# Column sums of block 3's norms: wide matmuls in four column groups instead of narrow ones

## The chip, the cores and the metric

The kernel runs on one core of a Trainium2 chip. The metric is the device time of one execution in microseconds (us). The core has a matmul engine (TensorE, PE in the profile; its weight loads are PEld), a vector engine (VectorE, DVE), a scalar engine (ScalarE, ACT), GpSimd (POOL) and SyncE (SP), which here only issues DMAs. The engines run side by side, each works through its own instructions in the order in which the program has them, and they wait for one another by semaphores. TensorE's results go to PSUM, eight banks of 128 partitions by 512 floats; everything else lies in SBUF.

## The reference

Three transformer blocks run one after the other on 512 tokens of width 1024, all in float32. The change touches the third. What of it matters here:

```python
def rms_norm_3(x, g):
    y = x32 * lax.rsqrt(jnp.mean(x32 * x32, axis=-1, keepdims=True) + EPS)
    return y.astype(x.dtype) * g

def layer_norm(x, g, b):
    mu = jnp.mean(x32, axis=-1, keepdims=True)
    xc = x32 - mu
    var = jnp.mean(xc * xc, axis=-1, keepdims=True)
    ...

    z = h @ w_in                                   # 1024 -> 4800
    c_q, c_kv, k_r, u_glu, gate_logits = jnp.split(z, IN_OFFSETS, axis=-1)
    q = (rms_norm_3(c_q, q_norm) @ w_uq)...        # c_q: 384 channels
    c_kv_n = rms_norm_3(c_kv, kv_norm)             # c_kv: 256 channels
    ...                                            # keys, values, 8 heads of causal attention
    u = a * jax.nn.sigmoid(b)                      # from u_glu
    u = lax.conv_general_dilated(u, conv_w, ...)   # 31 taps, depthwise, 1024 channels
    u = jax.nn.silu(layer_norm(u, conv_ln_g, conv_ln_b))
    y_conv = u @ w_pw2 + b_pw2
    merged = sigmoid(g_attn) * y_attn + sigmoid(g_conv) * y_conv
```

The program keeps these activations with channels in the partitions (tiles of 128 channels by 512 tokens), so a mean over channels is a sum over partitions and over tiles.

## The kernel before

The middle of block 3 is a mixture of several streams written as Python generators: `lat_p` (the 38 column blocks of `h @ w_in`; tile `pj`, 24 matmuls per block), `conv` (the 31 taps, each one VectorE instruction on a PSUM accumulator `cv`; result `uc`, L2146 and L2149), `mla_pre` (rope of the shared key, the two latent norms, the values `v`), `projs` and `heads` (per-head projections `sp`, scores `at`, transposed probabilities `pT`, outputs `ao`) and `conv_ln` (the LayerNorm after the convolution, then SiLU, written as the pair `uhh`/`uhl`). `run` interleaves them: each generator yields how many ns it thinks its last piece takes, and the one with the least sum goes next. A list scheduler under the language then orders each engine's instructions by readiness in its own model, so the order that runs is neither the text nor the yields alone.

A big product is three matmuls on float32r halves (`mm3`: high by high, high by low, low by high). The weights of `pj` come by DMA as `w`; ScalarE makes the high half `wh` (L442) and, in this stage, GpSimd the low half `wl` (L443), one unit for 12 matmuls.

The channel sums are made by `col_stat` (L2161). For each of the four groups of 128 tokens and each tile, it takes the 128x128 float32 piece of the tile as the stationary operand and a column pair of ones as the moving one, and accumulates into two columns of `cs`. That is four matmuls per tile: 8 for the key-value latents (2 tiles `ckn`), 12 for the query latents (3 tiles `cqn`), 32 for the sum of `uc` and 32 for the sum of its squares `ucq`. Each float32 matmul shows as two records in the trace. The sums land with tokens in the partitions, as 128x4.

For the latents (`col_rsqrt`, L2176) VectorE then turns the sum into mean plus epsilon (`cm`, L2186), GpSimd raises it to the power -1/2 (`cr`, L572), and `col_spread` (L2168) broadcasts the factor over all partitions by four matmuls (`cb`). VectorE multiplies each latent by `cb` (L2196). `conv_ln` does the same with its own lines (mean `mu` L2334, `cb`, subtraction L2337, squares L2342, `cm` L2346, `cr`, `cb`, product L2353).

Of the kernel before, what the change touches and what calls it, by code (L numbers as in the profile page):

```python
# [11 lines left out]
F32 = mybir.dt.float32  # L12
# [3 lines left out]
AF = mybir.ActivationFunctionType  # L16
OP = mybir.AluOpType
# [5 lines left out]
TT = 4  # L23
# [291 lines left out]
def kernel(ctx: ExitStack, tc: tile.TileContext, A, out):  # L315
    nc = tc.nc
    V, P, SC, PE = nc.vector, nc.gpsimd, nc.scalar, nc.tensor

    glob = ctx.enter_context(tc.tile_pool(name="glob", bufs=1))
# [5 lines left out]
    def T(name, dt=F32, n=512):  # L325
        return heap.tile([128, n], dt, name=name, tag="t")
# [4 lines left out]
    def SM(name, n, dt=F32):  # L331
        assert n <= 32
        return glob.tile([128, n], dt, name=name, tag="sm", bufs=24)

    def PS(name="ps"):
        return psum.tile([128, 512], F32, name=name, tag="ps")
# [10 lines left out]
    def con(n, i=0, w=None):  # L347
        o, ww = _COFF[n]
        w = ww if w is None else w
        return cons[:, o + i:o + i + w]  # L350
# [13 lines left out]
    def tok(t):  # L364
        return slice(128 * t, 128 * t + 128)
# [117 lines left out]
    for g in G3:  # L483
        n = (b + g + 1) // 2 - (b + 1) // 2
# [8 lines left out]
    def mm(ps, a, b, start, stop, **kw):  # L493
        PE.matmul(ps, a, b, start=start, stop=stop, **kw)  # L494
# [76 lines left out]
    def pow_half(y, m, n):  # L571
        P.tensor_tensor(y, m, mhalf[:, :n], op=OP.pow)  # L572
# [101 lines left out]
    for i, nm in enumerate(("c", "c_ctx")):  # L674
        cs = SM("cs", 8)
# [182 lines left out]
    for o in range(0, _NM, 512):  # L858
        a = T("mf")
# [447 lines left out]
    for e in range(NE):  # L1307
# [29 lines left out]
        for q in range(8):  # L1337
            w, rel = ws.raw()
            for kk in range(2):
                f = 2 * q + kk  # L1340
                p, c, j = f // 8, (f // 4) % 2, f % 4
# [9 lines left out]
        a = T("yg")  # L1351
# [803 lines left out]
    del xb, h2f, fp, first  # L2155
    table("sigmoid_and_others")

    ones = glob.tile([128, 2], F32, name="ones")
    P.memset(ones, 1.0)

    def col_stat(tiles, n):  # L2161

        ps = PS("cs")
        for t in range(TT):
            for i, a in enumerate(tiles):
                mm(ps[:, 2 * t:2 * t + 2], a[:, tok(t)], ones, t == 0 and i == 0,
                   t == TT - 1 and i == n - 1, skip_group_check=True)
        return ps[:, 0:8:2]  # L2168

    def col_spread(y):  # L2170

        ps = PS("cb")
        for t in range(TT):
            mm(ps[:, tok(t)], y[:, t:t + 1].to_broadcast([128, 128]), ident, True, True)
        return ps

    def col_rsqrt(tiles, width, eps, name):
        sq = []
        for a in tiles:
            b = T(name)  # L2180
            SC.activation(b, a, AF.Square)
            sq.append(b)
            yield 1400
        m, r = SM("cm", 4), SM("cr", 4)
        cs = col_stat(sq, len(sq))
        V.tensor_scalar(m, cs, 1.0 / width, eps, op0=OP.mult, op1=OP.add)  # L2186
        pow_half(r, m, 4)
        yield 3000
        res = col_spread(r)
        yield 1000  # L2190
        return res

    def latent_norm(tiles, width, gname, name, dst):
        rb_ = yield from col_rsqrt(tiles, width, EPS, name)
        for i, a in enumerate(tiles):
            V.scalar_tensor_tensor(a, a, vec(gname, i), rb_, op0=OP.mult, op1=OP.mult)  # L2196
            dst[i] = split(a, name, eng=P)
            yield 1500
# [130 lines left out]
    def conv_ln():  # L2329

        yield from slow(CV2, cv.rest())
        us_ = [uc[i] for i in range(8)]
        mu = SM("mu", 4)
        V.tensor_scalar(mu, col_stat(us_, 8), -1.0 / D, None, op0=OP.mult)  # L2334
        mb = col_spread(mu)
        for i in range(8):
# [3 lines left out]
        for a in us_:  # L2340
# [3 lines left out]
            yield 700  # L2344
        m, r = SM("cm", 4), SM("cr", 4)
        V.tensor_scalar(m, col_stat(sq, 8), 1.0 / D, EPS, op0=OP.mult, op1=OP.add)  # L2346
        del sq
        pow_half(r, m, 4)
# [106 lines left out]
```

## Time and profile before

| | us |
|---|---|
| median of 3 runs | 3111.37 (3109.46 to 3112.55) |
| the profiled execution | 3115.6 |
| its span in the trace | 3113.8 |
| TensorE busy | 2848.8 (91%) |
| VectorE busy | 1281.0 (41%) |
| ScalarE busy | 785.6 (25%) |
| GpSimd busy | 471.2 (15%) |

The profiled execution is 4.2 us over the median, and its span is 1.8 us shorter than its own time. The mixture of block 3 that holds all four norms lies between about 2325 and 2660 us of the span. Busy shares over the whole span say nothing of it; a stage is read by its own windows, where the granted clock of TensorE (1.00 is 2.4 GHz, 0.50 is 1.2 GHz) stands beside the busy time of each engine.

### The profile page before, as it was taken

The numbers are of one execution on the slowest core, as the hardware profiler recorded it, in microseconds if no ns is written. First come the engines' busy times: TensorE is split into PE (matmuls) and PEld (weight loads), VectorE is DVE, ScalarE is ACT, GpSimd is POOL, SyncE is SP. The second block draws the span as 40 slices with busy tenths as digits, with TensorE's granted clock in tenths as the row PEclk, the third lists the DMA queues.
The fourth block names the chain that finished last, engine by engine and source line by source line (L and its number), as shares of the span: only waits on it lengthen the run. The fifth ranks groups of instructions, "written<-read, shape, count | busy, mean of one in ns | idle before, by whom it ended". The sixth has DMA issues, their size and how long they took to land.

```text
span 3113.8 us, 35071 instructions
## 1 busy us (share of the span) xinstructions
PE 2848.8 (91%) x13954; PEld 1874.6 (60%) x13954; DVE 1281.0 (41%) x2363; ACT 785.6 (25%) x1623; POOL 471.2 (15%) x437
## 2 busy tenths in 40 slices
PE   7989979998888888887997899999998989999999
PEld 4866564442222222224875688888886766788887
DVE  4157551111112111114476653333798554453334
ACT  3233220100000000004332332223433233442322
POOL 1034230000000000002310111000253232310100
PEclk8989979999999999998998999999998989999999
DMA  6123538999999999994200122222322112422321
GB/s 259 68 82 129 219 140 337 392 419 420 419 420 419 419 420 420 420 419 187 83 27 1 69 95 95 102 95 88 125 95 84 65 38 88 176 82 102 108 83 67
DMA packets 99012, 605.29 MB, mean 194 GB/s; under 512 B 11008, under 2 KB 11136, under 8 KB 31008
## 3 DMA queue, kind: packets, MB, share of 16 engines
q1 hardware_dynamic: 98640, 602.39, 49.4%
q8 instruction: 110, 1.80, 0.2%
q0 software_dynamic: 208, 0.66, 0.1%
q14 instruction: 54, 0.44, 0.0%
HBM read 592.52 MB, written 10.49 MB: 194 GB/s over the span
## 4 chain that ended last, share of the span: by engine, by line
PE 60%; DMA 24%; DVE 11%; POOL 2%; issue 2%; ACT 2%; SPq 0%; POOLq 0%; DVEq 0%; ACTq 0%
PE pj L494 25%; PE pn L494 15%; DMA wb<-in_w_up_dram 9%; DMA w<-in_w_up_dram 5%; DMA wb<-in_w_down_dram 4%; PE pg L494 4%; DMA w<-in_w_down_dram 4%; DVE cv L2146 3%; PE py L494 2%; PE at L494 2%; PE sp L494 1%; PE xs L494 1%; PE pc L494 1%; PE ao L494 1%; PE kv L494 1%
## 5 line engine op out<-in xcount | busy, mean ns | idle before, releaser
L443 DVE TENSOR_TENSOR wl<-w,wh 128x512 fp32r<-128x512 f32 (+1 forms) x422 | 297.8, 749 | 204.1 <-ACT wh L442 156.1
L494 PE MATMUL pg<-wb,xs 128*64 128x512 f32 x1184 | 283.2, 607 | 38.4 <-DMA wb<-in_w_up_dram 21.4
L442 ACT CAST wh<-w 128x512 fp32r<-128x512 f32 (+1 forms) x516 | 292.0, 617 | 99.3 <-PE pn L494 94.4
L494 PE MATMUL pg<-w,xs 128*64 128x512 f32 x824 | 197.9, 604 | 28.6 <-DMA w<-in_w_up_dram 15.4
L572 POOL TENSOR_TENSOR r<-m,mhalf 128x1 f32<-128x1 f32 x46 | 31.0, 676 | 1213.1 <-DVE m L618 1206.6
L494 PEld LDWEIGHTS pg<-wb,xs 128*64 128x64 f32 x1184 | 76.9, 138 | 220.9 <-issue 126.9
L494 PE MATMUL pn<-wh,fh 128*128 128x512 f32 x432 | 168.1, 389 | 0.0
L494 PE MATMUL pn<-wh,fl 128*128 128x512 f32 x432 | 168.1, 389 | 0.0
L494 PE MATMUL pn<-wl,fh 128*128 128x512 f32 x432 | 168.1, 389 | 0.0
L494 PE MATMUL py<-wb,hidT 128*64 128x512 f32 x600 | 142.6, 601 | 26.4 <-DMA wb<-in_w_down_dram 26.4
L2146 DVE SCALAR_TENSOR_TENSOR cv<-glua,vecs,cv 128x482 f32<-128x482 f32 (+27 forms) x232 | 165.1, 736 | 4.0
L443 POOL TENSOR_TENSOR wl<-w,wh 128x512 fp32r<-128x512 f32 x94 | 124.9, 1347 | 166.7 <-ACT wh L442 153.3
L494 PEld LDWEIGHTS pg<-w,xs 128*64 128x64 f32 x824 | 52.4, 136 | 153.7 <-issue 84.4
L494 PE MATMUL pj<-h2fh,wh 128*128 128x512 f32 (+1 forms) x376 | 141.4, 378 | 2.5 <-ACT h2fh L644 2.5
L494 PE MATMUL pj<-h2fl,wh 128*128 128x512 f32 (+1 forms) x376 | 141.7, 377 | 0.0
L494 PE MATMUL pj<-h2fh,wl 128*128 128x512 f32 (+1 forms) x376 | 141.6, 377 | 0.0
L1335 DVE TENSOR_TENSOR sg<-sg,pg 128x512 f32<-128x512 f32 x16 | 11.0, 687 | 292.6 <-PE pg L494 292.6
L494 PE MATMUL pj<-h3h,wh 128*128 128x512 f32 (+1 forms) x336 | 129.6, 386 | 0.6 <-ACT h3h L644 0.6
L494 PE MATMUL pj<-h3l,wh 128*128 128x512 f32 (+1 forms) x336 | 127.0, 378 | 0.6 <-DVE h3l L646 0.6
L494 PE MATMUL pj<-h3h,wl 128*128 128x512 f32 (+1 forms) x336 | 126.8, 377 | 0.0
L1352 DVE SCALAR_TENSOR_TENSOR yg<-py,gsl,g2h 128x512 f32<-128x512 f32 x16 | 12.0, 751 | 271.5 <-PE py L494 271.5
L494 PE MATMUL py<-w,hidT 128*64 128x512 f32 x424 | 101.7, 602 | 20.9 <-DMA w<-in_w_down_dram 20.9
(610 smaller groups left out, 5736.4 us busy)
## 6 DMA issues: line engine op xcount, KB each, us to landing
wb<-in_w_gate_dram SPq DMA_DIRECT2D x75, 1024.0 KB, 19.9
wb<-in_w_down_dram SPq DMA_DIRECT2D x75, 1024.0 KB, 19.9
wb<-in_w_up_dram SPq DMA_DIRECT2D x73, 1024.0 KB, 19.9
w<-in_w_down_dram SPq DMA_DIRECT2D x53, 1024.0 KB, 19.9
w<-in_w_up_dram SPq DMA_DIRECT2D x52, 1024.0 KB, 19.9
w<-in_w_gate_dram SPq DMA_DIRECT2D x51, 1024.0 KB, 19.9
w<-in_w_in_dram SPq DMA_DIRECT2D x35, 1024.0 KB, 5.0
w<-in_w_ff_dram SPq DMA_DIRECT2D x30, 1024.0 KB, 4.8
```

The source lines that it names most:

```text
L442: SC.copy(hi, src)
L443: (eng or V).tensor_tensor(lo, src, hi.bitcast(F32), op=OP.subtract)
L494: PE.matmul(ps, a, b, start=start, stop=stop, **kw)
L572: P.tensor_tensor(y, m, mhalf[:, :n], op=OP.pow)
L1335: V.tensor_tensor(sg, sg, pu, op=OP.mult)
L1352: V.scalar_tensor_tensor(a, py, gsl[:, e:e + 1], g2h, op0=OP.mult, op1=OP.mult)
L2146: V.scalar_tensor_tensor(acc[:, sh:], a[:, :512 - sh], w[j], acc[:, sh:], op0=OP.mult, op1=OP.add)
```

## The change

`col_stat` makes the sums in two steps. First each tile is the moving operand (512 tokens wide) and a 128x32 tile of ones the stationary one; tile i writes the 32 PSUM partitions from 32*(i mod 4), so that four tiles use the four column groups of the array, and tiles 4 to 7 accumulate onto tiles 0 to 3. All 32 rows of a group hold the same sum. ScalarE copies `cs` to an SBUF tile `csum`. Then four narrow matmuls per sum, with `csum` stationary and `half2` moving (0.5 in every 16th partition, so two rows of each group count half each), bring the result to 128x4 as before, in a second bank (`cs2`). In `col_rsqrt` the step `cm` is split: ScalarE scales, GpSimd adds epsilon. One yield there is 5000 instead of 3000. `half2` is made once by GpSimd at the start of its queue.

```diff
-    ones = glob.tile([128, 2], F32, name="ones")
+    ones = glob.tile([128, 32], F32, name="ones")
     P.memset(ones, 1.0)
 
+    half2 = glob.tile([128, 2], F32, name="half2")
+    P.tensor_scalar(half2, con("eye16", 0, 1).to_broadcast([128, 2]), 0.5, None, op0=OP.mult)
+
     def col_stat(tiles, n):
         ps = PS("cs")
+        g = min(n, 4)
+        for i, a in enumerate(tiles):
+            c = 32 * (i % 4)
+            mm(ps[c:c + 32, :], ones, a, i < 4, i + 4 >= n, tile_position=(0, c))
+        a = T("csum")
+        SC.copy(a[:32 * g], ps[:32 * g])
+        ps = PS("cs2")
         for t in range(TT):
-            for i, a in enumerate(tiles):
-                mm(ps[:, 2 * t:2 * t + 2], a[:, tok(t)], ones, t == 0 and i == 0,
-                   t == TT - 1 and i == n - 1, skip_group_check=True)
+            mm(ps[:, 2 * t:2 * t + 2], a[:32 * g, tok(t)], half2[:32 * g], t == 0, t == TT - 1,
+               skip_group_check=True)
         return ps[:, 0:8:2]
...
         cs = col_stat(sq, len(sq))
-        V.tensor_scalar(m, cs, 1.0 / width, eps, op0=OP.mult, op1=OP.add)
+        SC.activation(m, cs, AF.Copy, scale=1.0 / width)
+        P.tensor_scalar(m, m, eps, None, op0=OP.add)
         pow_half(r, m, 4)
-        yield 3000
+        yield 5000
```

Up to the rope of the shared key, TensorE's instructions stand in the same order in both programs; from there the scheduler's order differs on every engine, down to the end of the mixture. Three places of it:

GpSimd, around the two latent factors. `lat` is the shared key's rope (its second line needs `ropeb` from VectorE), `cm` and `cr` the mean and the factor, `ckn` the normed key-value latents, `wl` the weights' low halves.

```order
 L443 TENSOR_TENSOR wl<-w,wh 128x512 x12
-L2208 TENSOR_TENSOR lat<-lat,cosB 128x512
-L2210 TENSOR_TENSOR lat<-lat,ropeb 128x512
+L2219 TENSOR_TENSOR lat<-lat,cosB 128x512
+L2221 TENSOR_TENSOR lat<-lat,ropeb 128x512
+L2197 TENSOR_SCALAR cm<-cm 128x4
 L572 TENSOR_TENSOR cr<-cm,mhalf 128x4
-L443 TENSOR_TENSOR cknl<-lat,cknh 128x512 x2
-L443 TENSOR_TENSOR wl<-w,wh 128x512 x3
+L443 TENSOR_TENSOR cknl<-lat,cknh 128x512
+L443 TENSOR_TENSOR wl<-w,wh 128x512 x2
+L443 TENSOR_TENSOR cknl<-lat,cknh 128x512
```

The new `cm` stands behind both rope lines, right ahead of `cr`, as `cr` did.

TensorE at the query latents, before: the last narrow sums, the projections behind them and the broadcast of the factor.

```order
L494 MATMUL cs<-ones,cqn 128x2 x10
L494 MATMUL pj<-h3h,wh 128x512
L494 MATMUL pj<-h3l,wh 128x512
L494 MATMUL pj<-h3h,wl 128x512
L494 MATMUL pj<-h3h,wh 128x512
L494 MATMUL pj<-h3l,wh 128x512
L494 MATMUL pj<-h3h,wl 128x512
L494 MATMUL cb<-cons,cr 128x128 x4
```

The same place now; the projections behind the second step go on to twelve before `cb` comes.

```order
L494 MATMUL cs<-cqn,ones 32x512 x2
L494 MATMUL pj<-h3h,wl 128x512
L494 MATMUL cs<-cqn,ones 32x512
L494 MATMUL cs_14791<-half_13698,csum 128x2 x4
L494 MATMUL pj<-h3h,wh 128x512
L494 MATMUL pj<-h3l,wh 128x512
L494 MATMUL pj<-h3h,wl 128x512
L494 MATMUL pj<-h3h,wh 128x512
L494 MATMUL pj<-h3l,wh 128x512
```

Between the last narrow sum and `cb` there are 12 projections instead of 6, and between the two latents' `cb` 60 instead of 36; the whole mixture has as many as before.

TensorE at the sum of squares of the LayerNorm (`sp` is a head's projection), before and now:

```order
L494 MATMUL cs<-ones,ucq 128x2 x7
L494 MATMUL pj<-h3h,wh 128x512
L494 MATMUL pj<-h3l,wh 128x512
L494 MATMUL cs<-ones,ucq 128x2 x25
L494 MATMUL pj<-h3h,wl 128x512
```

```order
L494 MATMUL cs<-ucq,ones 32x512 x8
L494 MATMUL pj<-h3h,wh 128x512
L494 MATMUL pj<-h3l,wh 128x512
L494 MATMUL pj<-h3h,wl 128x512
L494 MATMUL pj<-h3h,wh 128x512
L494 MATMUL cs_15797<-half_13698,csum 128x2 x4
L494 MATMUL sp<-cknh,wsh 128x512
```

Eight wide and four narrow matmuls stand where 32 narrow ones did, with four projections in between. At the sum of `uc` it is one `ao` and one projection that stand there. At the broadcast of the LayerNorm's factor, 15 `sp` and three score products (256, 384 and 512 tokens wide) that stood ahead of it before now stand behind it.

## Rows read from the trace of the kernel before

**Rows 1.** The page's head.

```profile
span 3113.8 us, 35071 instructions
```

**Rows 2.** Windows: stretch, length, busy us of each engine (instructions), granted clock, DMA.

```profile
2340.00:2350.00 10.00, 2.74 (x11) 2.55 (x12) 7.49 (x13) 0.00 (x0) 2.26 (x2) 0.50 0.00 0
2360.00:2370.00 10.00, 6.71 (x32) 5.48 (x32) 8.68 (x14) 0.10 (x1) 3.29 (x3) 0.62 0.31 120
...
2480.00:2500.00 20.00, 20.00 (x85) 15.70 (x83) 9.05 (x17) 7.15 (x15) 2.73 (x2) 0.87 0.06 20
...
2510.00:2520.00 10.00, 10.00 (x45) 9.81 (x46) 0.78 (x3) 0.24 (x1) 0.85 (x1) 0.50 0.00 0
...
2545.00:2565.00 20.00, 12.68 (x43) 7.99 (x44) 14.29 (x17) 14.44 (x29) 17.27 (x13) 0.88 0.00 0
```

**Rows 3.** TensorE's waits, 2325 to 2600: waiter, releaser, total, times, longest.

```profile
PE cb L494 <- POOL cr L572: 12.1, 2, 8.8
```

**Rows 4.** Timeline of GpSimd at the first factor: start, duration, instruction, idle before.

```profile
2344.95 1.26 POOL L2210 TENSOR_TENSOR lat<-lat,ropeb 128x512 f32<-128x512 f32 x1 [6.81 <-DVE ropeb L2209]
2346.17 1.04 POOL L572 TENSOR_TENSOR cr<-cm,mhalf 128x4 f32<-128x4 f32 x1
```

**Rows 5.** Timeline of VectorE at both factors and the value weights.

```profile
2345.36 0.15 DVE L2186 TENSOR_SCALAR cm<-cs 128x4 f32<-128x4 f32 x1
...
2349.37 0.75 DVE L2196 SCALAR_TENSOR_TENSOR lat<-lat,vecs,cb 128x512 f32<-128x512 f32 x1 [2.30 <-PE cb L494]
...
2365.47 0.16 DVE L2186 TENSOR_SCALAR cm<-cs 128x4 f32<-128x4 f32 x1
...
2377.23 1.79 DVE L443 TENSOR_TENSOR wvl<-wm,wvh 128x512 fp32r<-128x512 f32 x1 [1.93 <-ACT wvh L442]
```

**Rows 6.** Timeline of TensorE at the second factor.

```profile
2359.12 2.39 PE L494 MATMUL cs<-ones,cqn 128*128 128x2 f32 x20
...
2366.77 2.07 PE L494 MATMUL cb<-cons,cr 128*128 128x128 f32 x8 [3.29 <-POOL cr L572]
```

**Rows 7.** The chain of waits, 2320 to 2620: start, time on the chain, work.

```profile
2347.26 2.09 PE cb L494 x8
...
2368.85 12.73 PE pj L494 x48
2381.58 1.36 PE v L494 x6
2382.94 2.72 PE pj L494 x12
...
2466.72 0.86 PE rot L494 x2
...
2470.32 9.07 PE cs L494 x64
...
2506.60 1.65 PE cs L494 x14
2508.82 10.05 PE cs L494 x50
2518.87 4.29 PE pj L494 x10
```

**Rows 8.** Timeline of TensorE at block 1's modulation (`ada`: 32 stationary columns, four column groups).

```profile
356.06 0.39 PE L494 MATMUL pj<-hxh,wl 128*128 128x512 f32 x1
356.38 1.06 PE L494 MATMUL ada<-w,sil 128*32 128x512 f32 x8
357.38 0.49 PE L494 MATMUL o<-vn,zs 128*128 128x128 f32 x2
```

**Rows 9.** Groups by line and shape: count, busy us, mean ns, idle before.

```profile
L1422 POOL TENSOR_SCALAR ysh<-ya 128x1 f32<-128x1 f32 x11 | 2.4, 217 | 0.2
```

```profile
L2129 ACT COPY gt<-pj 128x512 f32<-128x512 f32 x16 | 9.4, 585 | 49.7 <-PE pj L494 49.7
```

## The prediction

> **What bounds the kernel now.** I read the windows of the stage first, then TensorE's waits, then the chain of waits, and last the timelines of single engines around the four norms. The windows show that TensorE is busy almost throughout, with three exceptions: 2340 to 2350 (2.74 of 10 us busy), 2360 to 2370 (6.71 of 10) and 2545 to 2565 (12.68 of 20) [rows 2]. They also show something that busy time hides: between 2510 and 2520 TensorE is busy for 10.00 of 10 us and yet the granted clock is 0.50, the 1.2 GHz level. What runs there are the narrow sums, 128x2 [rows 7]. The clock stands at 0.50 after the long wait (2340 to 2350), at 0.62 over the second wait, and at 0.87 after the first narrow sum of the LayerNorm [rows 2]. So both waits and long rows of narrow matmuls are followed by a stretch at the low level, in which all work runs at half speed.
>
> TensorE's waits name the two empty stretches: `cb` waits for the factor `cr` of GpSimd, 12.1 us in two waits, the longest 8.8 [rows 3]. The chain of waits shows what the sums cost on the path: 9.07 us for the 64 records of `uc`, 1.65 and 10.05 us for the 14 and 50 records of `ucq` [rows 7]. From 2368.85 to 2527 the chain is TensorE alone, so time taken off TensorE there shortens the stage until another engine is late. The sum below is made against the profiled execution, span 3113.8 [rows 1] and 3115.6 us in all; that is 4.2 us over the median of the runs, and I take the gain off the median.
>
> **Prices of the new operations.** Wide sums: block 1's modulation has the same shape (128x32 stationary, 512 wide, four column groups), and eight of its records, four matmuls, take 1.06 us at the full clock [rows 8]. Eight tiles make two such rounds, 2.1 us. If the groups ran one after the other, each matmul would take what a lone float32 product of this width takes, 0.86 us for two records [rows 7], and eight 6.9 us. I take 2.1, since rows 8 show the same form. Second step: 8 records of the narrow kind at 9.07/64 = 0.142 us, 1.1 us [rows 7]. The `csum` copy: as a 128x512 copy out of PSUM on ScalarE, 0.585 us [rows 9], with hand-overs about 0.8 us where nothing covers it. `cm` on GpSimd: between 0.22 (a 128x1 scalar operation [rows 9]) and 1.04 (the power of the same 128x4 [rows 4]); I take 0.25, the row of the same kind. `cm` on ScalarE: from 0.15 (VectorE's [rows 5]) to 0.585 (the full copy [rows 9]); I take 0.2.
>
> TensorE must also change between its full shape and the column groups. The row before `ada` starts at 356.06 and `ada` at 356.38, 0.32 us later where the pitch of such rows is 2.72/12 = 0.227 us, and the next product starts at 357.38, inside `ada`'s 1.06 us [rows 7, 8]: at most 0.1 us for a change. The Trainium skill, TensorEngine Tiling (Array Packing), section Key Properties, says that a change of tiling mode drains TensorE, which speaks against short visits to the column groups as this change makes them. By rows 8 the drain is a tenth of a microsecond, so five visits with their returns would cost under 1 us, and I leave them out of the sum.
>
> **Part A, the key-value factor: -0.2 us.** The change takes `cm` off VectorE, where it stood behind convolution taps. But that was not what ended last: `cm` ran at 2345.36 to 2345.51, and `cr` started only at 2346.17, when GpSimd had finished the rope line of 2344.95 to 2346.21 [rows 4, 5]. That line waited 6.81 us for `ropeb`, which VectorE makes behind the taps [rows 4]. The order shows the same taps ahead of `ropeb` and both rope lines still ahead of the new `cm`. So the 8.8 us wait stays, and GpSimd's new step lengthens it by 0.25 us (0.15 to 1.0). The wide sums and the copy lie inside this wait and cost nothing; were the wait gone, they would cost about 0.86 + 0.8 + 1.1 against the 1.8 of the old ones. TensorE's clock falls as before. What does change: VectorE no longer stands still 2.30 us for `cb` [rows 5], since seven taps now come ahead of the first product, so the convolution is some 2 us earlier.
>
> **Part B, the query factor: +5.8 us.** Before, `cm` ran at 2365.47 behind taps though the sums were done by 2361.5, and TensorE waited 3.29 us [rows 5, 6]. Now ScalarE and GpSimd need 0.2 + 0.25 + 1.04 us and hand-overs, about 2 us, behind the second step, and 12 projections, 2.72 us [rows 7], stand in between: +3.3. The clock: 48 projections took 12.73 us, four times the 12 at full clock would be 10.88 [rows 7], and of 2360 to 2370 at 0.62 another 4 us of work ran at the low level [rows 2], together 1.85 + 1.5: +3.3 if the clock now stays up. The sums: 20 records in 2.39 us and four more, 2.9 us [rows 6], against one round, one lone tile, the open wait for `csum` and the second step, 0.9 + 0.9 + 0.8 + 1.1 = 3.7: -0.8. The wait comes back if the low weight halves of the 24 projections that moved ahead are late. They stand on GpSimd between the two factors, four units for 48 matmuls, and TensorE has three units in hand there, so I cost them at nothing; without that cover it is the 3.3 again.
>
> **Part C, the sum of `uc`: +8.3 us.** 9.07 us become 2.1 + 1.1 = 3.2, and `csum` is covered but for 0.2 by one `ao` and one projection: +5.7. The stretch of 2480 to 2500 at 0.87 has 26% of its 20 us, 5.2 us, at the low level [rows 2], in which half the work is lost: +2.6.
>
> **Part D, the sum of `ucq`: +10.5 us.** 1.65 + 10.05 = 11.7 become 3.2; four projections, 0.9 us, cover `csum`: +8.5. The ten projections behind took 4.29 us and at 0.227 would take 2.3 [rows 7]: +2.0.
>
> **Part E, behind the LayerNorm: +4 us (0 to 7.3).** In 2545 to 2565 TensorE had work for 12.68 of 20 us while ScalarE, VectorE and GpSimd made `uh` [rows 2]. The 15 `sp` and three score products that now come behind the factor, 15 x 0.227 = 3.4 us and an estimated 1 to 1.5 each by the 0.86 of a lone float32 product [rows 7], together some 7 us, fill that. I take about half, since they too need softmax steps of the same engines.
>
> **Part F, new waits: -2 us (0 to -10).** TensorE comes to the values `v` about 6 us earlier, VectorE only 2. The first low half of the value weights ended at 2379.02 and `v` began at 2381.58, 2.6 us of slack [rows 5, 7]; 6 - 2 - 2.6 leaves 1.4 us of waiting, and I add 0.6 for like places in the heads; the far end takes three waits of the second factor's 3.3 us [rows 6]. `half2` is one GpSimd step of 0.2 us at the start of its queue, ahead of powers that wait for VectorE: nothing, 0.2 if they did not.
>
> Sum: -0.2 + 5.8 + 8.3 + 10.5 + 4 - 2 = 26.4. 3111.4 - 26.4 = **3085 us**. The likeliest case by itself runs from 3080 to 3094, with part E from 7.3 down to 0 and part F from 0 to -7.
>
> **Rivals.**
> 1. *The lead on TensorE is given back, because the clock falls all the same or because VectorE's convolution sets the start of the LayerNorm.* For it: the clock also fell while TensorE was counted busy, and four sums still have narrow records; VectorE is busy 8.68 of 10 us in 2360 to 2370 [rows 2]. Against it: eight narrow records are a sixteenth of the two long rows, and the chain from 2368.85 on is TensorE's. Then B's and C's and D's clock terms (3.3 + 2.6 + 2.0) and E (4) go: 26 - 12 = 14, 3097 us.
> 2. *The change does not do what it says: the column groups run one after the other.* Then each eight-tile sum costs 6.9 instead of 2.1 and the three-tile one 0.9 more: 26 - 10.5 = 15, 3096 us. Against it stand rows 8.
> 3. *Slower: ScalarE's queue becomes the bound.* Each sum now goes through ScalarE, four `csum` and two `cm`; while ScalarE stands waiting for TensorE's sums, the softmax, `wh` and `wsh` behind it stand too, and TensorE then waits for those. If each of the six places costs TensorE what the second factor cost it, 3.3 us of waiting and 3.3 us of low clock (part B), that is 40 us, and the time is 3111 - 26 + 40 = 3125. It decides from 26/6 = 4.3 us per place on. Against it: ScalarE is busy 7.15 of 20 us in 2480 to 2500 [rows 2], and at the two LayerNorm sums the order has work for TensorE between the wide sums and the second step.
> 4. *More than expected: part F is nothing and the whole of 2545 to 2565 fills.* 26.4 + 2 + 3.3 = 31.7, and up to 5 us more where small waits went with the low clock: about 3077 us, 3075 at the far end.
>
> **Chances.** Likeliest case 0.62; first rival 0.14; second 0.05; third 0.05; fourth 0.14. The range 3070 to 3102 holds the first, second and fourth as well, and leaves out the third and the tails. A measurement of this kernel tells 0.2%, 6.2 us, from no change. Faster by more: all but the third rival and the bad tail of the first, 0.91; within 0.2%: 0.05; slower: 0.04.
>
> **What would show it.** Right: TensorE still waits about 9 us for `cr` at the first factor, with GpSimd's rope line ending just before `cm`; no wait at the second `cb`; eight wide sums in about 2.1 us; a granted clock near 1.00 from 2370 to the stage's end; less idle time of TensorE ahead of the first `pj` from `uhh`. Wrong: the first wait is short (then `ropeb` came earlier than the order lets me think), the clock is below 0.9 around the two LayerNorm sums (rival 1), wide sums at 0.86 us each (rival 2), or new TensorE waits for ScalarE's `probT`, `wh` or `csum` of several us each (rival 3).

## The result, and the profile after

| | before | after |
|---|---|---|
| median of 4 runs, us | 3111.2 (3109.5 to 3112.6) | 3088.6 (3086.7 to 3091.7) |
| ratio, 95% interval | | 0.9924 (0.9912 to 0.9936) |
| profiled execution / its span | 3115.6 / 3113.8 | 3089.25 / 3087.5 |
| mean granted clock | 0.965 | 0.973 |
| TensorE busy | 2848.8 | 2825.3 |

The change wins 22.6 us; 26.4 were forecast. The page's head after, beside [rows 1]:

```profile
span 3087.5 us, 34890 instructions
```

The windows of the stage after, columns as in [rows 2]. The stage now begins 3.5 us earlier in the trace, and the LayerNorm's two sums stand 16 and 25 us earlier:

```profile
2340.00:2350.00 10.00, 5.81 (x20) 5.00 (x21) 9.93 (x17) 1.17 (x3) 3.03 (x4) 0.57 0.00 1
2360.00:2370.00 10.00, 9.33 (x42) 7.43 (x41) 6.62 (x10) 2.95 (x6) 3.77 (x4) 0.83 0.38 131
2480.00:2500.00 20.00, 20.00 (x96) 13.46 (x95) 10.87 (x27) 5.55 (x14) 2.31 (x2) 1.00 0.28 95
2500.00:2520.00 20.00, 17.23 (x64) 9.78 (x63) 15.85 (x45) 11.59 (x28) 5.41 (x5) 1.00 0.04 14
2520.00:2540.00 20.00, 12.86 (x44) 8.41 (x43) 9.16 (x10) 8.82 (x19) 14.54 (x11) 0.83 0.00 0
```

The clock of 0.50 and 0.87 around the LayerNorm's sums has gone (the second sum lies in 2480 to 2500, at 1.00). But 2500 to 2540 is now the place where TensorE stands idle: 30.09 of 40 us busy, against 2545 to 2565 in [rows 2]; and behind that idle time the clock falls (0.83 in 2520 to 2540).

TensorE's waits after, 2325 to 2680, where [rows 3] had 12.1 us for `cr`:

```profile
PE cb L494 <- POOL cr L572: 8.2, 1, 8.2
PE ao L494 <- ACT probT L1793: 7.3, 4, 6.1
...
PE cs L494 <- ACT csum L2173: 1.4, 2, 0.7
```

The second wait for `cr` is gone, the first is still there. In the tail of the LayerNorm TensorE now waits 6.1 us in one piece for `probT`; before, the longest such wait was 3.4 us (same stretch, kernel before):

```profile
PE ao L494 <- ACT probT L1793: 3.7, 2, 3.4
```

GpSimd at the first factor after, beside [rows 4]. The rope line still waits for `ropeb`, and the new `cm` stands right behind it:

```profile
2341.41 1.26 POOL L2221 TENSOR_TENSOR lat<-lat,ropeb 128x512 f32<-128x512 f32 x1 [6.77 <-DVE ropeb L2220]
2342.76 0.24 POOL L2197 TENSOR_SCALAR cm<-cm 128x4 f32<-128x4 f32 x1
2343.08 1.05 POOL L572 TENSOR_TENSOR cr<-cm,mhalf 128x4 f32<-128x4 f32 x1
```

TensorE's sums after (timeline), beside [rows 6, 7]: the query latents with the factor behind them, then `uc`, then `ucq`. No row but that of the query's `csum` has idle time ahead of it:

```profile
2358.07 1.05 PE L494 MATMUL cs<-cqn,ones 128*32 128x512 f32 x4
2359.48 1.04 PE L494 MATMUL cs<-cqn,ones 128*32 128x512 f32 x2
2361.19 1.05 PE L494 MATMUL cs<-half,csum 96*128 96x2 f32 x8 [0.67 <-ACT csum L2173]
2366.53 1.05 PE L494 MATMUL cb<-cons,cr 128*128 128x128 f32 x8
...
2454.68 1.92 PE L494 MATMUL cs<-uc,ones 128*32 128x512 f32 x16
2457.52 0.95 PE L494 MATMUL cs<-half,csum 128*128 128x2 f32 x8
...
2481.84 2.32 PE L494 MATMUL cs<-ucq,ones 128*32 128x512 f32 x16
...
2485.15 0.95 PE L494 MATMUL cs<-half,csum 128*128 128x2 f32 x8
```

**One yardstick for what follows.** The same work ahead of the stage ends up to 8 us earlier or later from one execution to the next, so that spans and medians of variants 3 us apart say little. I count each trace from the first copy of a latent out of PSUM on ScalarE, here of before and of after, to the end of its span:

```profile
2307.88 0.59 ACT L2125 COPY lat<-pj 128x512 f32<-128x512 f32 x1 [2.46 <-PE pj L494]
```

```profile
2304.37 0.59 ACT L2125 COPY lat<-pj 128x512 f32<-128x512 f32 x1 [2.46 <-PE pj L494]
```

3113.8 - 2307.88 = 805.9 and 3087.5 - 2304.37 = 783.1: 22.8 us, which agrees with the medians (22.6). It is one execution per kernel. Kernels with the same order up to a mark agree there within some tenths, or within 1.6 us where TensorE's clock drops for a moment at the second factor in the one and not in the other (0.83 in 2360 to 2370 after, 1.00 in the same stretch of the spread kernel). Up to the end of the span a single trace says less. From the first `pj` with `uhh` and `wl` on, the kernels "wide for LayerNorm alone" and "old yield" of the table below have equally many records and the same idle time, 11.7 and 11.6 us, but TensorE is busy 3.7 us longer in the second, where the clock is lower (0.97 against 0.99 over the first 210 us; TensorE alone: stretch, length, busy, clock, DMA):

```profile
2540.64:3089.19 548.55, 536.89 (x2404) 0.99 0.28 100
2533.41:3085.60 552.19, 540.58 (x2404) 0.99 0.28 100
```

So differences of 2 to 4 us in the column "end" are not shown by one trace. The ratio of the runs, each against runs of the kernel before from the same time, has an interval of about 0.0013 to either side, 4 us. In this table "tail" runs from `cb` of the LayerNorm's factor to the first `pj` with `uhh` and `wl`; all times are from that first copy.

| kernel | first, second factor `cb` | sum of `uc` | LayerNorm's `cb` | tail | end | median of runs | ratio of runs |
|---|---|---|---|---|---|---|---|
| before | 39.4, 58.9 | 162.3 | 218.6 | 37.1 | 805.9 | 3111.2 |  |
| after | 39.8, 62.2 | 150.3 | 185.6 | 45.9 | 783.1 | 3088.6 | 0.9924 |
| wide for LayerNorm alone | 39.3, 58.9 | 162.5 | 199.0 | 38.4 | 785.9 | 3089.7 | 0.9931 |
| latents' way alone | 39.8, 60.4 | 149.0 | 202.1 | 49.4 | 803.1 | 3112.0 | 0.9997 |
| old yield | 39.8, 57.1 | 158.9 | 195.4 | 38.4 | 785.9 | 3089.1 | 0.9924 |
| one column group | 39.8, 61.6 | 149.8 | 195.5 | 46.0 | 793.1 | 3099.2 | 0.9960 |
| rope behind first norm | 33.4, 57.1 | 158.5 | 195.0 | 38.1 | 782.4 | 3085.1 | 0.9924 |
| low half on VectorE | 39.8, 62.1 | 150.2 | 185.6 | 46.0 | 783.5 | 3087.1 | 0.9927 |
| affine on ScalarE | 39.8, 62.2 | 150.4 | 185.7 | 45.9 | 783.5 | 3088.7 | 0.9929 |
| three combined | 33.4, 56.4 | 159.4 | 195.9 | 37.4 | 781.8 | 3087.9 | 0.9923 |
| spread tail | 39.8, 60.7 | 148.8 | 184.1 | 50.2 | 776.9 | 3082.1 | 0.9899 |
| rope behind both | 33.4, 51.9 | 154.5 | 188.1 | 44.0 | 786.6 | 3091.9 | 0.9930 |
| both of these | 33.4, 51.9 | 152.9 | 186.5 | 48.6 | 776.7 | 3077.3 | 0.9886 |
| spread, latents as before | 39.4, 58.9 | 162.5 | 198.9 | 42.3 | 779.0 | 3081.7 | 0.9900 |

Two marks can be compared directly only where the order ahead of them is the same; a mark that comes earlier may mean that work has been put behind it.

### The profile page after: what moved, and what is told of

Its sections match the earlier page's. It is cut to its first block, busy times and chain, and to the rows that moved or that the text cites. A ratio compares the mean times of both kernels' runs of the same rounds, so it can differ in the third digit from the quotient of the medians.

```text
span 3087.5 us, 34890 instructions
## 1 busy us (share of the span) xinstructions
PE 2825.3 (92%) x13860; PEld 1847.5 (60%) x13860; DVE 1278.5 (41%) x2361; ACT 788.3 (26%) x1629; POOL 472.6 (15%) x440
## 4 chain that ended last, share of the span: by engine, by line
PE 60%; DMA 24%; DVE 10%; ACT 2%; issue 2%; POOL 2%; SPq 0%; DVEq 0%; POOLq 0%; ACTq 0%
PE pj L494 25%; PE pn L494 15%; DMA wb<-in_w_up_dram 9%; DMA w<-in_w_up_dram 5%; DMA w<-in_w_down_dram 4%; PE pg L494 4%; DMA wb<-in_w_down_dram 4%; DVE cv L2146 2%; PE py L494 2%; PE at L494 2%; PE sp L494 1%; PE xs L494 1%; PE pc L494 1%; PE ao L494 1%; PE kv L494 1%
## 5 line engine op out<-in xcount | busy, mean ns | idle before, releaser
L2146 DVE SCALAR_TENSOR_TENSOR cv<-glua,vecs,cv 128x507 f32<-128x507 f32 (+27 forms) x232 | 164.4, 735 | 4.2
L443 POOL TENSOR_TENSOR wl<-w,wh 128x512 fp32r<-128x512 f32 x94 | 125.2, 1351 | 150.4 <-ACT wh L442 135.6
L494 PE MATMUL py<-w,hidT 128*64 128x512 f32 x424 | 102.4, 606 | 19.9 <-DMA w<-in_w_down_dram 19.9
```

What stands on the lines that cost most here:

```text
L443: (eng or V).tensor_tensor(lo, src, hi.bitcast(F32), op=OP.subtract)
L2146: V.scalar_tensor_tensor(acc[:, sh:], a[:, :512 - sh], w[j], acc[:, sh:], op0=OP.mult, op1=OP.add)
```

## The experiments

### What the two hunks bring apart

The wide sums for the LayerNorm alone: `col_rsqrt` calls a copy of the old `col_stat`, and has its old lines.

```diff
+    def col_stat_narrow(tiles, n):
...
-        cs = col_stat(sq, len(sq))
-        SC.activation(m, cs, AF.Copy, scale=1.0 / width)
-        P.tensor_scalar(m, m, eps, None, op0=OP.add)
+        cs = col_stat_narrow(sq, len(sq))
+        V.tensor_scalar(m, cs, 1.0 / width, eps, op0=OP.mult, op1=OP.add)
         pow_half(r, m, 4)
-        yield 5000
+        yield 3000
```

> The wide sums are kept at the LayerNorm alone; the two latents have the narrow sums, VectorE's cm and the old order again. Theory (parts C and D carry the gain, 18.8 us in the forecast, part B 5.8): the wait of some 3 us at the second factor is back, the clock is near 1.00 from 2400 us to the norm's end, and the gain over the kernel before is 17 us (14 to 20). Rival (what the latents win is given back later, since VectorE sets when the LayerNorm starts): the gain is that of the whole change, 22 to 23 us.

Ratio 0.9931 (0.9918 to 0.9943), which is 17.7 to 25.5 us; by the trace 20.0. The second wait is back, as expected:

```profile
2362.15 2.08 PE L494 MATMUL cb<-cons,cr 128*128 128x128 f32 x8 [3.63 <-POOL cr L572]
```

The clock is 1.00 from 2370 to 2520. The trace's 20.0 is at the edge of the theory's range, 2.8 us short of the whole change; by the runs (0.9931 against 0.9924, with overlapping intervals) next to nothing is missing, as the rival has it. The runs don't tell the two apart.

The counterpart: the kernel before with the second hunk alone, so that the narrow sums stay everywhere.

```diff
-        V.tensor_scalar(m, cs, 1.0 / width, eps, op0=OP.mult, op1=OP.add)
+        SC.activation(m, cs, AF.Copy, scale=1.0 / width)
+        P.tensor_scalar(m, m, eps, None, op0=OP.add)
         pow_half(r, m, 4)
-        yield 3000
+        yield 5000
```

> The narrow sums stay everywhere; only the factor's way through ScalarE and GpSimd and the later product with it are changed. Theory: the second wait goes, the LayerNorm's sums take 9 and 11.7 us with the clock falling to 0.50 as before, and the gain is part B's, 5 to 6 us (less what the VectorE convolution that now comes earlier gives or takes). Rival (the new lead is eaten by the convolution on VectorE): 0 to 2 us.

Ratio 0.9997 (0.9988 to 1.0006): no change that can be told. By the trace 2.8 us, which is within what a single trace leaves open. The 50 narrow records of `ucq`, 8.13 us from 2493.63 on, and the work right behind them lie in these stretches, where TensorE is busy throughout and the clock falls all the same:

```profile
2490.00:2500.00 10.00, 10.00 (x68) 9.65 (x66) 2.10 (x3) 1.37 (x3) 0.79 (x1) 0.82 0.32 107
2500.00:2510.00 10.00, 10.00 (x39) 7.95 (x39) 2.14 (x8) 1.45 (x4) 1.02 (x1) 0.67 0.13 32
```

The second factor has no wait (`cb` at 2365.82 without idle), so that B does what the prediction said at its own place; but at most half of it reaches the end. By the trace the two kernels add up: 20.0 + 2.8 = 22.8.

### What removes the second wait

The changed kernel with the old yield in `col_rsqrt`.

```diff
-        yield 5000
+        yield 3000
         res = col_spread(r)
```

> The changed kernel, but with the latents' product with the factor put back to where it stood in TensorE's order (3000 in place of 5000). Theory A (it is the engines: the factor takes 2 us of steps and VectorE's taps are out of its way): the second wait shrinks from 3.3 us to below 2 us, and the time is 0 to 3 us above the changed kernel's. Theory B (it is the 12 projections that stand between): the wait is 2 to 3 us and the clock falls behind it, 4 to 6 us above the changed kernel.

TensorE at the second factor in this kernel:

```profile
2353.10 1.05 PE L494 MATMUL cs<-half,csum 96*128 96x2 f32 x8 [0.67 <-ACT csum L2173]
...
2356.83 1.05 PE L494 MATMUL cb<-cons,cr 128*128 128x128 f32 x8
```

No wait at `cb`. But the order is only in part the old one: 36 projections stand between the two `cb` again, yet 12 of them, as in the changed kernel and not 6 as before, stand between the query's sums and `cb`. So this run does not part theory A from theory B. The rows of GpSimd in the changed kernel do, as an estimate:

```profile
2362.86 1.04 POOL L572 TENSOR_TENSOR cr<-cm,mhalf 128x4 f32<-128x4 f32 x1
```

The sums there end at 2362.24, the factor is done at 2363.90, 1.7 us later, and `cb` starts only at 2366.53; before, `cb` came 5.3 us behind the sums [rows 6]. Six projections fewer, 1.4 us, would still leave no wait, so the shorter way over the engines is enough by itself in the changed kernel. No run shows it without the 12 projections.

The time is 3089.1, as the changed kernel's (by the trace 2.8 us more, in which the low clock behind the tail, shown above, has its part). At the first `pj` with `uhh` and `wl` this kernel is 3.6 us ahead of the one where the LayerNorm alone is wide, with the same work ahead of it; this lead is what the latents' part wins without the new yield, and at the end of the trace nothing of it is left. The table shows something else. With the old yield the tail is 38.4 us, as where the LayerNorm alone is wide; with the new one it is 45.9. The 7.5 us of difference are about the length of the heads' work that 5000 moves behind the factor (some 7 us in the prediction's part E). TensorE stands idle for 7.7 us of the tail with the old yield and 9.9 with the new. So that work fills no idle time there; it makes the tail longer by itself.

### What the column groups are worth

```diff
-        g = min(n, 4)
+        g = 1
         for i, a in enumerate(tiles):
-            c = 32 * (i % 4)
-            mm(ps[c:c + 32, :], ones, a, i < 4, i + 4 >= n, tile_position=(0, c))
+            mm(ps[:32, :], ones, a, i == 0, i == n - 1, tile_position=(0, 0))
```

> The changed kernel, but all tiles of a sum go through one column group, one behind the other; csum is then 32 partitions high. Theory (groups run beside each other): eight tiles take 8 x 0.86 = 6.9 us in place of 1.9 to 2.3, three tiles 2.6 in place of some 1.7, so the time is about 10 us above the changed kernel's, 3098 to 3100. Rival (the groups change little, the width of the rows is what helps): within 3 us of the changed kernel.

```profile
2453.88 7.05 PE L494 MATMUL cs<-uc,ones 128*32 128x512 f32 x16
...
2486.44 7.05 PE L494 MATMUL cs<-ucq,ones 128*32 128x512 f32 x16
```

```profile
2450.00:2470.00 20.00, 19.91 (x72) 10.36 (x73) 7.16 (x18) 3.58 (x9) 2.52 (x2) 1.00 0.15 52
2480.00:2500.00 20.00, 20.00 (x80) 12.05 (x79) 2.86 (x6) 7.52 (x15) 2.31 (x2) 1.00 0.19 67
```

7.05 us for eight tiles (6.9 expected), and 793.1 against 783.1: 10.0 us, as expected. The groups run beside each other in the changed kernel (1.92 and 2.32). The clock stays at 1.00, although these sums take nearly as long as the narrow ones did (7.05 against 9.07 [rows 7]): it is not their brevity that keeps it up.

This run also parts the clock from the shorter work. At the full clock a narrow record takes 0.118 us (1.65 for 14 [rows 7]), so 64 of them would take 7.6; one column group with its second step takes 7.05 + 1.05, some 8, and saves no work at all. From the start of the sum of `uc` to the LayerNorm's `cb`, in the kernel with the latents' way alone, in this one and in the changed one (TensorE alone, columns as above; 131 records besides the sums in each):

```profile
2454.37:2507.51 53.14, 53.14 (x259) 0.81 0.15 50
2453.88:2499.57 45.69, 45.69 (x179) 1.00 0.17 58
2454.68:2489.99 35.31, 35.31 (x179) 1.00 0.21 75
```

From the first to the second 7.4 us go, with no less work: that is the clock. From the second to the third 10.4 go, at one clock: that is the column groups.

### The first wait

The changed kernel with `rope(kr, kr)` and its yield behind the key-value norm.

```diff
+        yield from latent_norm([lat[3], lat[4]], 256, "kv_norm_3", "ckn", ckp)
         kr = lat[5]
         rope(kr, kr)
         yield 4000
-        yield from latent_norm([lat[3], lat[4]], 256, "kv_norm_3", "ckn", ckp)
```

> The changed kernel, but the rope of the latents' sixth tile is issued behind the key-value norm instead of ahead of it, so that GpSimd's step of cm and its power no longer stand behind a rope line that waits for VectorE. Theory (part A: the rope line holds the factor): the first wait of 8.2 us shrinks to 2 to 3 us (csum 0.7, cm 0.17 and 0.24, the power 1.05, hand-overs), the clock stays up, and the time is 5 to 9 us below the changed kernel's. Rival (the lead is eaten behind it, as that of part B was by the LayerNorm's tail): the wait shrinks all the same, but the time falls by 0 to 3 us.

The waits of this kernel, 2320 to 2500:

```profile
PE cb L494 <- POOL cr L572: 3.1, 2, 1.7
PE sp L494 <- ACT wsh L442: 2.1, 2, 1.1
PE pj L494 <- POOL wl L443: 1.7, 1, 1.7
PE v L494 <- DVE wvl L443: 1.6, 1, 1.6
```

The first wait falls from 8.2 to at most 1.7 us and `cb` comes 6.4 us earlier: the rope line did hold the factor. But the end is only 0.7 us earlier by the trace, and the ratio of the runs is the changed kernel's, 0.9924 (the profiled executions, 4.2 us apart, have 3.5 of that ahead of the stage). All the waits of TensorE until 2500 come to 12.6 us; they were 10.6. The rival holds: what is won here is waited for again, at low weight halves and values. VectorE, busy 9.93 of 10 us in 2340 to 2350 after, has no room to make them earlier.

Moving the rope behind both norms:

```diff
+        yield from latent_norm([lat[3], lat[4]], 256, "kv_norm_3", "ckn", ckp)
+        yield from latent_norm([lat[0], lat[1], lat[2]], 384, "q_norm_3", "cqn", cqp)
         kr = lat[5]
         rope(kr, kr)
         yield 4000
-        yield from latent_norm([lat[3], lat[4]], 256, "kv_norm_3", "ckn", ckp)
-        yield from latent_norm([lat[0], lat[1], lat[2]], 384, "q_norm_3", "cqn", cqp)
```

> The changed kernel with the rope behind both latents' norms, so that it stands ahead of neither factor. Theory: both factors come in some 2 us, no wait of TensorE for cr is over 2 us, and the second factor keeps the 6 us lead that the first one wins; 4 to 6 us below the changed kernel. Rival (VectorE is busy 9.8 of 10 us in this stretch, and all that TensorE wins there it waits for again at the low weight halves and the values): the lead is gone by the sum of uc, 0 to 2 us below the changed kernel.

Both factors are early, but `v` now waits 2.50 us for VectorE in one place, and the time is 3.5 us longer by the trace:

```profile
2377.14 0.50 PE L494 MATMUL v<-wvl,cknh 128*128 128x512 f32 x1 [2.50 <-DVE wvl L443]
```

The theory falls, and the rival was still too kind by the trace; by the runs (0.9930 against 0.9924) the two kernels can't be told apart. The wait for `v` is not all of it: from the first copy to the end TensorE idles 32.6 us here and 33.1 in the changed kernel, but is busy 754.1 against 750.1 us.

### What makes the tail long

Each of two edits to the changed kernel takes load off one engine in the tail. `uhl` on VectorE instead of GpSimd:

```diff
-            P.tensor_tensor(l, y, h.bitcast(F32), op=OP.subtract)
+            V.tensor_tensor(l, y, h.bitcast(F32), op=OP.subtract)
```

> The changed kernel, but the low halves of the LayerNorm's output are subtracted on VectorE instead of GpSimd. Theory (part E: VectorE's scalar_tensor_tensor steps, 0.68 us alone and 1.3 to 1.7 us each while GpSimd subtracts, set the tail): they fall to 0.68 us, the stretch from the factor to the first pj from uhh shrinks from 44.5 to about 40 us, and the time is 3 to 5 us lower. Rival (the softmax steps of the moved heads set it, or VectorE's 8 x 0.68 us more take the place): within 2 us of the changed kernel.

And the LayerNorm's scale and offset on ScalarE:

```diff
-            V.tensor_scalar(y, y, vec("conv_ln_g_3", i), vec("conv_ln_b_3", i), op0=OP.mult, op1=OP.add)
+            SC.activation(y, y, AF.Identity, scale=vec("conv_ln_g_3", i), bias=vec("conv_ln_b_3", i))
```

> The changed kernel, but the LayerNorm's scale and offset (eight 128x512 steps of 0.53 us on VectorE) go to ScalarE. Theory (VectorE is what the tail waits for): the tail gets some 3 us shorter, and so does the time. Rival (ScalarE's queue, in which a softmax copy stood behind the casts and made TensorE wait 6.1 us, is what the tail waits for): the wait grows and the time is 0 to 4 us longer.

Both leave everything as it was: tails of 46.0 and 45.9 us, ends 0.4 us later, ratios 0.9927 and 0.9929. In the first, VectorE's `uc` steps do fall to 0.67 us, but the low halves stand among them on VectorE, and TensorE still waits 5.89 us for `probT`. The affine steps all lie ahead of the stretch that decides. Both theories fall.

Three edits together (rope behind the key-value norm, low half on VectorE, `yield 3000`):

> The changed kernel with the rope behind the key-value norm, the low halves on VectorE and the latents' product back in its old place in the order (3000 in place of 5000), so that the head's work isn't moved behind the LayerNorm's factor. If the three are independent and the tail no longer takes what is won ahead of it: 8 to 12 us below the changed kernel. If the tail takes it: 0 to 4 us below.

781.8, 1.3 us less than after, ratio 0.9923: nothing adds. Here the second factor waits again, since on GpSimd the rope line and three low weight halves now stand ahead of its `cm` (timelines of GpSimd and of TensorE):

```profile
2356.88 1.28 POOL L2221 TENSOR_TENSOR lat<-lat,ropeb 128x512 f32<-128x512 f32 x1 [6.54 <-DVE ropeb L2220]
2358.12 3.70 POOL L443 TENSOR_TENSOR wl<-w,wh 128x512 fp32r<-128x512 f32 x3
2361.91 0.23 POOL L2197 TENSOR_SCALAR cm<-cm 128x4 f32<-128x4 f32 x1
```

```profile
2363.32 2.07 PE L494 MATMUL cb<-cons,cr 128*128 128x128 f32 x8 [5.57 <-POOL cr L572]
```

What stands ahead of `probT` in the changed kernel shows on ScalarE, with VectorE's row beside it:

```profile
2523.06 0.62 ACT L2377 CAST uhh<-uc 128x512 fp32r<-128x512 f32 x1 [0.33 <-DVE uc L2375]
2524.74 0.62 ACT L2377 CAST uhh<-uc 128x512 fp32r<-128x512 f32 x1 [1.06 <-DVE uc L2375]
2526.41 0.62 ACT L2377 CAST uhh<-uc 128x512 fp32r<-128x512 f32 x1 [1.05 <-DVE uc L2375]
2526.93 0.58 ACT L1793 COPY probT<-pT 128x512 f32<-128x512 f32 x1
```

```profile
2521.36 5.01 DVE L2375 SCALAR_TENSOR_TENSOR uc<-th,uc 128x512 f32<-128x512 f32 x3
```

The transposes that this `probT` copies were done by 2521.5. The copy stands behind three casts, each of which waits for VectorE. So it is the order on ScalarE's queue, and the next edit changes that: the last eight steps of the LayerNorm are spaced wider.

```diff
-            yield 1300
+            yield 2400
         ready["uh"] = uh
```

> The changed kernel, but the last eight steps of the LayerNorm are spaced wider in the issue order (2400 in place of 1300 between them), so that two fewer of the uhh casts stand ahead of the probT copy on ScalarE, and more of the heads' work ahead of the first pj from uhh. Theory (part E failed because the heads' softmax copies stand in ScalarE's queue behind casts that wait for VectorE): the wait of 6.1 us for probT shrinks to 2 to 3 us, and the time falls by 3 to 5 us. Rival (VectorE has so much to do in this stretch that TensorE waits for it in any order): the wait comes back at other places, the time stays within 2 us.

```profile
2519.78 0.62 ACT L2377 CAST uhh<-uc 128x512 fp32r<-128x512 f32 x1 [0.91 <-DVE uc L2375]
...
2520.98 0.62 ACT L2377 CAST uhh<-uc 128x512 fp32r<-128x512 f32 x1 [0.17 <-DVE uc L2375]
2521.50 0.58 ACT L1793 COPY probT<-pT 128x512 f32<-128x512 f32 x1
```

```profile
2522.13 1.38 PE L494 MATMUL ao<-probT,v 128*128 128x512 f32 x2 [2.85 <-ACT probT L1793]
```

The wait falls to 2.85 us, and the time to 3082.1 (ratio to before 0.9899, 0.9884 to 0.9914), 6.5 us below the changed kernel by the medians and 6.2 by the trace, of which 1.5 are the clock at the second factor and 4.7 come behind the LayerNorm's factor. The tail itself is longer (50.2), but holds more of the heads' work, which is then not left for later; TensorE idles 7.2 us of it instead of 9.9, at a mean granted clock of 0.97 instead of 0.93. This theory stands.

Together with the rope behind both norms:

> Both of the last two edits: the rope behind both norms, the LayerNorm's steps spaced wider. If they add: 7 to 11 us below the changed kernel by the theories of both, 0 to 3 us by the rivals.

3077.3 us (ratio 0.9886, 0.9872 to 0.9899), the fastest of all: 11.3 us below the changed kernel, 34 below before. By the trace the stage is no shorter than with the spacing alone (776.7 against 776.9); its first copy comes 4.7 us earlier, ahead of which TensorE has as many records in both kernels (10550) and is busy 2067.7 against 2075.0 us. That is more than the chance of one trace: the four runs lie at 3076.2 to 3078.2, those of the spacing alone at 3080.0 to 3083.0. What makes that part shorter stays open, so I count only the 6.4 us of the stage for the edits.

Last, the spacing with the latents as before, to see whether part B shows in full where the tail is eased (the "spaced kernel" of the expectation is the one with the spacing alone):

> The LayerNorm's wide sums and its wider spacing, but the two latents as before (narrow sums, VectorE's cm, old order): the last but one experiment's spacing with part B taken away. Counted from the first lat copy on ScalarE to the end of the span, the spaced kernel took 776.9 us. Theory (part B wins 5.6 us at the second factor and the tight tail took half of it): with the tail eased it shows in full, so this one takes 782 to 783 us. Rival (part B's lead is lost between the factor and the LayerNorm, or is worth 3 us in any case): 779 to 780. If it is lost in full where the tail is eased: 777.

779.0 against 776.9: as the rival has it, by the trace part B is worth 2.1 us here and 2.8 with the tight tail; the runs (0.9900 against 0.9899) show nothing of it. So the lost half of B is not in the tight tail alone. In the other direction this kernel ends 6.9 us ahead of "wide for LayerNorm alone": the spacing wins as much where no heads' work has been moved, since the wait for `probT` of 3.4 us stood there before the change too. In this kernel TensorE waits 12.3 us for `cr`, as before, but for `probT` at most 0.6 at a time:

```profile
PE cb L494 <- POOL cr L572: 12.3, 2, 8.8
PE ao L494 <- ACT probT L1793: 2.4, 6, 0.6
```

Summed from 2320 to 2640, the waits of TensorE are 19.4 us here and 19.7 in the spread kernel with part B. Where they go shows in TensorE's idle time by stretches, in us (length of a stretch less busy time):

| kernel | first factor's `cb` to the sum of `uc` | tail | behind the tail |
|---|---|---|---|
| before | 4.6 | 7.9 | 11.7 |
| wide for LayerNorm alone | 4.7 | 7.8 | 11.7 |
| after | 1.0 | 9.9 | 12.6 |
| old yield | 3.1 | 7.7 | 11.6 |
| spread, latents as before | 4.7 | 4.2 | 11.3 |
| spread tail | 1.0 | 7.2 | 11.8 |

With the latents' part 3.7 us less of idle time stand at the factors and 3.0 more in the tail and behind it; with the spacing 3.6 less and 3.5 more, in the waits for `probT` and `kn`. So the idle time that part B takes away comes back nearly whole, and what can be left of B is the clock.

## Why the prediction was right, and where it was not

The sign, the size and the likeliest case were right; 22.6 of 26.4 us came. By its parts:

- **Price of the wide sums** (2.1 us for eight tiles, from [rows 8]): 1.92 and 2.32. The second step (1.1): 0.95. `csum` 0.59 (0.585), `cm` on GpSimd 0.24 (0.25). All from rows of the same shape elsewhere in the trace. The Trainium skill, TensorEngine Tiling (Array Packing), section Key Properties, has a change of tiling mode drain TensorE; the sums with such a change on both sides came out 0.2 us to either side of the price without one, so that no cost of it is seen here.
- **A (-0.2), the first wait stays:** right. 8.2 us, GpSimd's rope line just ahead of `cm`. Moving the rope showed that it is the rope line, and also that taking this wait away by itself wins next to nothing (0.7 us by the trace, 0.9924 as before the move by the runs), which the prediction left open.
- **B (+5.8):** right at its own place, no wait at the second `cb`. But it was booked as if TensorE's lead ran through to the end. By the trace 2.8 us are left there, alone or on top of the rest, and by the runs that is not told from nothing. The 3.7 us of idle time that went at the factors came back in the tail and behind it. The step "+3.3, since 12 projections stand in between" had the right result; by the rows the shorter way over the engines would have been enough, but no run has it without the 12 projections.
- **C and D (8.3 + 10.5 = 18.8):** 20.0, from the kernel in which only they act. The sums went from 9.07 to 1.92 + 0.95 and from 11.7 to 2.32 + 0.95, 14.6 us; the other 5.4 are put down, by subtraction, to the clock behind them, for which 2.6 + 2.0 had been set. But the prediction took the old sums as they stood, partly at the low level (10.05 for 50 records is 0.201 each, against 0.118 at the full clock [rows 7]). At the full clock the two would have taken some 15.1 us and not 20.8, so that of the 14.6 another 5.7 are the clock. By this estimate about 9 us are shorter work and 11 the clock: a total near the forecast, with more than twice the share of the clock.
- **E (+4, 0 to 7.3):** this step failed, in its sign. The prediction said that the heads' work moved behind the factor would fill TensorE's idle time. It took the half off "since they too need softmax steps of the same engines", and that was the whole matter: TensorE's idle time in the tail was 7.9 us before and is 9.9 after, 2 more and not 4 less. The softmax copies stand in ScalarE's queue among the casts, the tail grew from 38.4 (old yield) to 45.9 us, and TensorE waits 6.1 us for one `probT` where it waited 3.4. That is one of the signs that the prediction named for being wrong, and of those for being right "less idle time ahead of the first `pj` from `uhh`" did not come.
- **F (-2):** at `v` no wait is listed in the changed kernel; 1.6 us came up at `kn`. B, E and F were to bring 5.8 + 4 - 2 = 7.8 and bring 2.8 by the trace.
- **Rivals:** of the first, the part "the lead is given back" came true for B, though at ScalarE and not at the convolution. Around the sums the clock did not fall (1.00 in 2480 to 2500); it fell behind the wait for `probT`. The second is excluded by the run with one group, which cost 10.0 us (10.5 in the prediction). The third is in the trace on a small scale: ScalarE's queue cost one wait of 6.1 us, 2.7 more than before, not six of them.

Summed over 2320 to the end, TensorE waits 26.3 us before and 26.0 after. TensorE's busy time fell by 23.5 us, from 2848.8 to 2825.3. The gain is therefore shorter work and the clock, about half each by the estimate above, and none of it is waiting. That the total came within 4 us of the forecast owes something to luck: the clock gave more than it was booked for, the shorter work less, and E gave nothing.

## What to carry to other kernels

Long rows of matmuls with two moving columns cost twice here, in time and in the clock during and behind them; a sum over partitions with ones stationary and the data moving, spread over column groups, cost about 30% of the time here. A wait taken away where a second engine is busy nearly throughout (here VectorE at 9.9 of 10 us) must be followed to the end before it is booked: here it came back at the next two or three places. Work moved into idle time did not help, because its own copies queued behind the very steps for which the idle time was waiting; spacing those steps was worth more (5 to 7 us) than taking either wait at a factor away (at most 3 us, and nothing). A price read off a row contains the clock that the row ran at: the same work elsewhere in the trace at the full clock says what of it is work.

## What was not expected of the hardware

- The clock went with the form of the float32 sums, and not with their length or with TensorE's busy time. `uc` and `ucq` as 128x2 rows, each with a 128x128 stationary piece: 0.67 to 0.82 in the kernel with the latents' way alone and 0.50 before [rows 2]. As 128x512 rows over one 128x32 stationary tile, in one column group for 7.05 us: 1.00. TensorE counted as busy for 19.9 or all of every 20 us in them. Whether it is the width of what moves or the change of what is stationary, no run tells.
- VectorE's `scalar_tensor_tensor` of 128x512 takes 0.68 us alone and 1.67 each (5.01 for three) while GpSimd subtracts beside it. Taking this away did not shorten the stage.
- The same work ahead of the stage ended between 2299.6 and 2307.9 us in the traces of these kernels, so that two single executions need a mark inside the trace; and behind a mark, the same 2404 records with the same idle time took TensorE 536.9 and 540.6 us, by the clock alone.
